# Experts' weights in pieces of 2 MB with 16 KB contiguous on a partition, in place of 1 MB with 8 KB

## The chip, the cores and the metric

The kernel runs on one core of one Trainium2 chip. Its time is the device time of one execution in microseconds (us). A profile is one further execution, taken with the hardware profiler on. In what follows MB means 1024 x 1024 bytes where a piece is meant (the profile's GB/s are decimal).

## The reference

One inference step of a small hybrid network on 256 tokens (128 of a prompt, 128 of a sample), model width 1024, one layer, all in float32. First a mixer (one input projection, a state-space scan in two directions, a convolution branch, gates, an output projection), then a mixture of 32 experts, of which each token takes 4:

```python
logits = t @ w_router + b_router                    # t: 256 x 1024
top_vals, top_idx = lax.top_k(logits, 4)
probs = softmax(top_vals)
combine = (one_hot(top_idx, 32) * probs[..., None]).sum(axis=1)
for e in range(32):
    g, u = split(t @ w_gu[e] + b_gu[e], 2)          # w_gu[e]: 1024 x 2048, 8 MB
    g = minimum(g, 7.0)
    u = clip(u, -7.0, 7.0)
    act = (u + 1.0) * g * sigmoid(1.702 * g)
    out = act @ w_down[e] + b_down[e]               # w_down[e]: 1024 x 1024, 4 MB
    acc = acc + combine[:, e:e + 1] * out
```

and at last a normalisation of both streams. The experts' weights are 32 x 12 = 384 MB and are read once.

## The kernel before

**Stages.** The mixer comes first. Its weights, some 80 MB, are loaded in pieces whose contiguous runs are 1, 2 or 8 KB; each is split in two for a product in three parts. Then the router picks the experts, and a loop `expert(e)` goes over the 32 experts. TensorE's part of that loop is written by hand in order; the other engines' order and SP's order of loads come from a scheduler.

**One expert.** A place in a list of up to 64 tokens is worked out for each expert. `gather` (line 1200) picks the tokens of two experts by products with 0/1 matrices, so that the contraction index lies on partitions: chunk `k` of eight holds 128 of the 1024 inputs. `expert_up` (line 1223, tile `e..pgu`) multiplies chunk `k` by the 128 rows of `w_gu` that belong to it, for k = 0 to 7, four products of 512 columns for each k. `expert_act` makes the activation, `transposed` (line 1272, `e..pat`) puts it on partitions in eight chunks, and `down_products` (line 1283, `e..py`) multiplies these by the rows of `w_down`. `scatter_pair` and `add_pair` bring two experts' results back to their tokens. In iteration e the order on TensorE is: down of e-1, overflow of e, up of e, then either `add_pair` or the next `gather`. `overflow` runs only for an expert with more than 64 tokens, in passes of 32 tokens (tiles `r..` and `q..`); in the profile it ran once, for expert 11.

**Pieces and places.** Twelve pieces of 1 MB make an expert: pieces 0 to 7 are 128 rows of `w_gu` each (8 KB of a row on each partition), pieces 8 to 11 are 256 rows of `w_down` (two rows of 4 KB, contiguous, on each partition). There are `NSLOT = 22` places of 1 MB, taken in turn: piece n goes where piece n-22 was, and its load waits until TensorE has read that piece. 19 places lie in memory that the mixer frees bit by bit (`open_slots`), two where a mixer buffer `y` was, one where `xn` was. `early_pieces` starts ten loads during the mixer's last products. All loads of weights are issued by SP, one after the other, so a load that waits holds back every load behind it; `load_pieces(12 * e + NSLOT)` (line 1424) sets how far ahead they are written. Down products of piece c read `w[8 + k // 2][:, k % 2]`, up products `w[k][:, 0]`.

Of the kernel before, what the change touches and what calls it, by code (L numbers as in the profile page):

```python
# [28 lines left out]
OVER = 32  # L29
NSLOT = 22  # L30
NBLOCK = 113
# [32 lines left out]
def hybrid_step(ctx, tc, A):  # L64
# [296 lines left out]

    mx, npc, ready, two = [], [0], {}, [None]
    npc_ins, last_early = [None], [None]
    w_gu, w_dn = A["w_gu"], A["w_down"]

    def next_slot(name):
        npc[0] += 1
        return slot((npc[0] - 1) % NSLOT, name)

    def slot(i, name):  # L370
        if i == NSLOT - 1:
            return keep.tile([P, 2 * D], F32, name=name, tag="xn", bufs=1)
        if i < NSLOT - 3:
            return mx[i].tile([P, 2 * D], F32, name=name, tag="w")
        if i == NSLOT - 3:
            two[0] = ypool.tile([P, 2, 2 * D], F32, name=name, tag="y")
        return two[0][:, i - (NSLOT - 3)]

    def load_piece(e, c, t=None):
        if t is None:  # L380
            t = ready.pop((e, c), None)
            if t is not None:
                npc[0] += 1
                return t
            t = next_slot(f"w{e}_{c}")
        if c < 8:
            npc_ins[0] = nc.sync.dma_start(t, w_gu[0, e, c * P:(c + 1) * P, :])
            return t.unsqueeze(1)

        t = t.rearrange("p (k n) -> p k n", k=2)  # L390
        nc.sync.dma_start(t, w_dn[0, e, (c - 8) * 256:(c - 7) * 256, :].rearrange("(p k) n -> p k n", k=2))
        return t

    def open_slots(n):
        for i in range(len(mx), len(mx) + n):
            mx.append(ctx.enter_context(tc.tile_pool(name=f"mx{i}", bufs=1, side="right")))

    def early_pieces(n):

        with tc.issue_after(last_load[0].ins):  # L400
            for _ in range(n):
                i = early.pop(0)
                ready[divmod(i, 12)] = load_piece(*divmod(i, 12), slot(i, f"w{i // 12}_{i % 12}"))
                last_early[0] = npc_ins[0]


    early = [0, 1, 2, NSLOT - 3, NSLOT - 2, *range(3, NSLOT - 3)]

    loads = [0]
    pieces = {}  # L410

    def load_pieces(n):

        for i in range(loads[0], min(n, 12 * NE)):
            pieces.setdefault(i // 12, []).append(load_piece(i // 12, i % 12))
        loads[0] = max(loads[0], n)

    first_in = []

    def weight_blocks():  # L420
# [34 lines left out]
        for c in range(8):  # L455

            w = load(f"wso{c}", w_so[:, c // 4 * KC:(c // 4 + 1) * KC, c % 4 * 256:(c % 4 + 1) * 256])
            early_pieces({2: 1, 3: 2, 5: 2}.get(c, 0))
            yield from w
        for c in range(4):  # L460

            w = piece(ring(), f"wcf{c}", w_cf[:, c // 2 * 4:c // 2 * 4 + 4, c % 2 * 512:(c % 2 + 1) * 512], [P, 4, 512])
            early_pieces(c // 3)
            w = w.rearrange("p k (i n) -> p i k n", n=P)
            yield w[:, 0:2]
            yield w[:, 2:4]
        for c in range(4):
            with tc.issue_after(last_early[0].ins) if c == 1 else ExitStack():
                w = load(f"wo{c}", w_o[:, :, c * 256:(c + 1) * 256])
            early_pieces(c // 3)  # L470
            yield from w
# [467 lines left out]

    open_slots(3)  # L940

# [4 lines left out]
    def ssd_out(hf):  # L946
        for j in range(KC):
            o = pos[j // 2][:, j % 2 * T:(j % 2 + 1) * T]
            proj(o, yhl[hf][:, 0], yhl[hf][:, 1], first=hf == 0 and j % 2 == 0, last=hf == 1)
            if hf == 1:  # L950
                V.scalar_tensor_tensor(gt[:, j, :], gt[:, j, :], 1.0, o, op0=ALU.add, op1=ALU.mult)
            if hf == 1 and j == 1:
                early_pieces(2)
            yield

    run(ssd_out(0))
    sy[0].close()
    open_slots(2)
    ssd_q.append(split_conf())
# [4 lines left out]
    sy[1].close()  # L964
    open_slots(2)
    early_pieces(1)
# [20 lines left out]
    sc.close()  # L987
    open_slots(1)
    for j in range(KC):
# [148 lines left out]
    weights.close()  # L1138
    open_slots(NSLOT - 5 - len(mx))
    hp = ctx.enter_context(tc.tile_pool(name="hp", bufs=1, side="right"))  # L1140
# [23 lines left out]

    open_slots(NSLOT - 3 - len(mx))
    def add_gated(k, s, x):
# [44 lines left out]
    def expert_up(e, xg, w, banks, m, after=None, half_way=None):  # L1211


        nq = P // m
        wd = D // nq
        for k in range(KC):
            if half_way and k == KC // 2 - 1:
                half_way()
            with tc.issue_after(after.ins) if after else ExitStack():
                for i in range(2):  # L1220
                    for q in range(nq):
                        c0 = i * D + q * wd
                        PE.matmul(banks[i][m * q:m * q + m, 0:wd], xg[:, k, :], w[k][:, 0, c0:c0 + wd],  # L1223
                                  start=(k == 0), stop=False, skip_group_check=True)
        for i in range(2):
            for q in range(nq):
                c0 = i * D + q * wd
                PE.matmul(banks[i][m * q:m * q + m, 0:wd], sel3[:, e:e + 1].to_broadcast([96, m]), b3[:, c0:c0 + wd],
# [36 lines left out]
    def transposed(gm, name, m, tag="aT", bufs=1):  # L1265

        wd = D * m // P
        pat = bank("E", name + "pat", 1)[:, 0:wd]
        aT = sm.tile([P, 512], F32, name=name + "aT", tag=tag, bufs=bufs)[:, 0:wd]
        for c in range(wd // P):  # L1270
            c0 = c // 2 * 256
            PE.transpose(pat[:, c * P:(c + 1) * P], gm[:, c0 + c % 2:c0 + 256:2], ident)  # L1272
        S.copy(aT, pat)
        return [aT[:, a:a + m] for a in (k * P % wd + k * P // wd * m for k in range(KC))]

    def down_products(at, w, py, m, swap):
# [62 lines left out]
    def overflow_pass(e, w, over, n, xo):  # L1339
# [14 lines left out]
        for c in range(wd // P):  # L1354
            PE.transpose(pxt[:, c * P:(c + 1) * P], xs[:, c * P:(c + 1) * P], ident)
        S.copy(xo, pxt[:, 0:wd].rearrange("p (c q s) -> p q c s", q=nq, s=m))
# [48 lines left out]
    def expert(e):  # L1405
        nonlocal w, last, mores
        w = pieces.setdefault(e, [])
        if e <= 1:
            load_pieces(12 * e + 12)
        if e % REGS == 0:  # L1410
# [8 lines left out]
        if e > 1:  # L1419
# [3 lines left out]

            load_pieces(12 * e + NSLOT)
        overflow(e, w, more)
# [23 lines left out]
    def finale():  # L1449
# [131 lines left out]
```

## Time and profile before

| | |
|---|---|
| Median of 3 runs | 1448.36 us (1447.45 to 1451.06) |
| The profiled execution's own time | 1453.59 us |
| Its span in the profile | 1451.8 us |
| TensorE busy | 1343.5 us (93%) |
| DMA over the span | 349 GB/s, 506.57 MB (decimal) |
| Loads of `w_gu` and `w_down` | 256 and 128, 1024 KB each |

The profiled execution lies 5.2 us above the median of the runs; sums below are made against its span, and carried to the median as differences. [...] The row of 40 slices shows the stages: the mixer up to about slice 13, then the experts, in which DMA moves some 417 GB/s slice after slice.

### The profile page before, as it was taken

The page shows a single profiled execution, that of the slowest core. Times are in us where ns is not written, and L with a number is a line of the kernel's source. Part 1 is how long each engine was busy: PE and PEld are TensorE (multiplying, and loading weights), DVE is VectorE, ACT ScalarE, POOL GpSimd, SP SyncE. Part 2 cuts the span into 40 slices and gives each one's busy share as a digit, 9 for nine tenths or more (in the row PEclk, how much of TensorE's full clock was granted, in tenths as well). Part 3 has the DMA queues.
Part 4 walks back from the last instruction along what each step waited for, and adds up shares of the span by engine and source line. Part 5 has one row for each costly group of instructions (what it writes and reads, how often), then busy time and mean ns, then how long its engine had stood idle before and what let it go on. Part 6 is the DMA issues. An engine that isn't in the chain of part 4 may idle for free. (4 is left out here: it accounts for less than half of the span.)

```text
span 1451.8 us, 21213 instructions
## 1 busy us (share of the span) xinstructions
PE 1343.5 (93%) x8531; PEld 791.8 (55%) x8531; DVE 591.1 (41%) x1265; ACT 337.5 (23%) x636; POOL 107.4 (7%) x121
## 2 busy tenths in 40 slices
PE   6898999999999899999999799999999998999986
PEld 3887888898999543443434344344344333343332
DVE  4855789898776322132122212213213213132123
ACT  2534565565664110000000000001001000000001
POOL 1112313431002100000000000000000000000001
PEclk9999999999999899999999999999999999999997
DMA  9996656556878799999999999999999999999991
GB/s 367 264 277 167 222 205 238 202 212 207 312 289 290 275 402 418 418 418 418 417 418 419 414 416 418 417 418 419 418 418 417 417 412 417 414 412 417 413 404 40
DMA packets 108625, 506.57 MB, mean 349 GB/s; under 512 B 9634, under 2 KB 36898, under 8 KB 54178
## 3 DMA queue, kind: packets, MB, share of 16 engines
q1 hardware_dynamic: 105570, 497.72, 88.0%
q10 hardware_dynamic: 2880, 6.60, 1.3%
q8 instruction: 99, 1.62, 0.5%
q14 instruction: 76, 0.62, 0.1%
HBM read 498.26 MB, written 5.64 MB: 347 GB/s over the span
## 5 line engine op out<-in xcount | busy, mean ns | idle before, releaser
L291 DVE TENSOR_TENSOR wl<-win,wh 128x1024 fp32r<-128x1024 f32 (+1 forms) x84 | 100.7, 1210 | 37.8 <-ACT wh L290 29.8
L290 ACT CAST wh<-win 128x1024 fp32r<-128x1024 f32 (+1 forms) x84 | 84.0, 1010 | 73.2 <-PE pbc L318 16.8
L1475 POOL TENSOR_TENSOR sql<-sql 128x256 f32<-128x256 f32 x3 | 2.2, 729 | 952.9 <-PE pcl L1462 952.5
L702 POOL TENSOR_TENSOR m<-m_half,adt 128x512 fp32r<-128x512 f32 x32 | 42.5, 1346 | 89.3 <-PE pss L705 89.3
L318 PE MATMUL pxs<-hT,wh 128*128 128x256 f32 x256 | 37.5, 291 | 0.0
L318 PE MATMUL pz<-hT,wh 128*128 128x256 f32 x256 | 37.3, 291 | 0.0
L318 PE MATMUL pgt<-hT,wh 128*128 128x256 f32 x256 | 36.0, 287 | 0.9 <-ACT wh L290 0.9
L318 PE MATMUL pbc<-hT,wh 128*128 128x256 f32 x256 | 35.6, 287 | 0.0
L318 PEld LDWEIGHTS pxs<-hT,wh 128*128 128x128 f32 x256 | 32.5, 190 | 3.6 <-issue 2.8
L318 PE MATMUL pso<-yhl,wh 128*128 128x256 f32 x256 | 34.1, 284 | 0.0
L318 PEld LDWEIGHTS pz<-hT,wh 128*128 128x128 f32 x256 | 33.0, 193 | 1.8 <-issue 1.8
L318 PEld LDWEIGHTS pgt<-hT,wh 128*128 128x128 f32 x256 | 32.4, 191 | 2.9 <-issue 1.9
L318 PEld LDWEIGHTS pbc<-hT,wh 128*128 128x128 f32 x256 | 32.1, 190 | 1.9 <-issue 1.7
L318 PEld LDWEIGHTS pso<-yhl,wh 128*128 128x128 f32 x256 | 32.1, 192 | 0.0
L318 PE MATMUL pglu<-hT,wh 128*128 128x256 f32 x192 | 25.9, 285 | 0.0
L318 PEld LDWEIGHTS pglu<-hT,wh 128*128 128x128 f32 x192 | 24.0, 191 | 0.7 <-issue 0.5
L215 PE MATMUL pm<-ada,sc__170 128*32 128x512 f32 x80 | 14.7, 792 | 10.0 <-DMA ada<-in_w_ada 10.0
L291 DVE TENSOR_TENSOR wl<-wso,wh 128x1024 fp32r<-128x1024 f32 x16 | 19.4, 1218 | 7.5 <-ACT wh L290 7.3
L685 ACT ACTIVATE gd<-gm,dtT 128x128 f32<-128x128 f32 x64 | 20.8, 414 | 4.3 <-DVE gm L676 4.3
L686 DVE SCALAR_TENSOR_TENSOR gd<-gm,dtT,gd 128x128 f32<-128x128 f32 x64 | 20.9, 374 | 1.6 <-ACT gd L685 1.2
L563 PE MATMUL pcv<-im,wst 128*32 128x144 f32 x256 | 12.1, 333 | 9.5 <-DMA im<-dru 5.9
L290 ACT CAST wh<-wso 128x1024 fp32r<-128x1024 f32 x16 | 16.7, 1046 | 14.4 <-PE pso L318 10.8
(1026 smaller groups left out, 2639.4 us busy)
## 6 DMA issues: line engine op xcount, KB each, us to landing
w<-in_w_gu SPq DMA_DIRECT2D x256, 1024.0 KB, 19.9
w<-in_w_down SPq DMA_DIRECT2D x128, 1024.0 KB, 19.9
win<-in_w_in_pack SPq DMA_DIRECT2D x38, 1024.0 KB, 5.6
ada<-in_w_ada SPq DMA_DIRECT2D x10, 1024.0 KB, 10.2
wso<-in_w_ssd_out SPq DMA_DIRECT2D x8, 1024.0 KB, 7.2
im<-dru SPq DMA_DIRECT2D x16, 312.0 KB, 9.2
wcf<-in_w_conf_out SPq DMA_DIRECT2D x4, 1024.0 KB, 8.8
wo<-in_w_o SPq DMA_DIRECT2D x4, 1024.0 KB, 9.2
```

The lines of the kernel that those rows point to most:

```text
L215: PE.matmul(out[32 * j:32 * j + 32, :], sc_[:, 4 * r + j, 6 - 2 * c:38 - 2 * c], part[:, j, :], start=(start and r == 0), stop=(stop and r ...
L290: S.copy(hi[:, ks, 0:m], w[:, ks])
L291: V.tensor_tensor(lo[:, ks, 0:m], w[:, ks], hi[:, ks, 0:m], ALU.subtract)
L318: last_wo[0] = PE.matmul(out, w[:, k, 0:n], m[:, k, :], start=first and i == 0, stop=last and i == len(order) - 1, skip_group_check=True)
L563: PE.matmul(pc[32 * b:32 * b + 32, h * NOUT:(h + 1) * NOUT], wst[:, 4 * h + b, j, :], im[:, 8 * (t % 2) + 4 * h + b, 4 * j:4 * j + NOUT], ...
L685: S.activation(gd[s][:, h, :], gm[:, 0, s, :], AF.Copy, scale=dtT[:, 0, s, c0:c0 + 1])
L686: V.scalar_tensor_tensor(gd[s][:, h, :], gm[:, 1, s, :], dtT[:, 0, s, 32 + c0:33 + c0], gd[s][:, h, :], op0=ALU.mult, op1=ALU.add)
L702: G.tensor_tensor(m4[d], m_half[:, d, None, None, :].to_broadcast([P, 2, 4, 64]), ac[d], ALU.mult)
L1475: G.tensor_tensor(sq[:, 0], sq[:, 0], sq[:, k], ALU.add)
```

## The change

A unit is now 2 MB, and an expert has six: four of 256 rows of `w_gu`, two of 512 rows of `w_down`. Partition p holds rows 2p and 2p+1 of the unit (or rows 4p to 4p+3 of `w_down`), which are 16 KB contiguous in HBM and on the partition. There are `NUNIT = 11` places of 2 MB. One of them, place 10, is made of two separate places of 1 MB, so that a unit that falls on it (17 of the 192) is loaded in two halves, 8 KB contiguous each. The last two units of the last expert are loaded in two halves each, too. Nine MB are started early instead of ten. Since a partition now holds neighbouring rows, the contraction index is dealt out otherwise: `gather` reads every second column of `h2`, `transposed` every fourth of the activation, and the overflow pass deals its quarters in the order 0, 2, 1, 3 and transposes with eight products of 64 x 64 in place of two of 128 x 128.

```diff
-NSLOT = 22
+NUNIT = 11
...
-    def load_piece(e, c, t=None):
...
-        if c < 8:
-            npc_ins[0] = nc.sync.dma_start(t, w_gu[0, e, c * P:(c + 1) * P, :])
-            return t.unsqueeze(1)
-
-        t = t.rearrange("p (k n) -> p k n", k=2)
-        nc.sync.dma_start(t, w_dn[0, e, (c - 8) * 256:(c - 7) * 256, :].rearrange("(p k) n -> p k n", k=2))
-        return t
...
+    def place(i, name, h):
+
+        if i < NUNIT - 2:
+            return mx[i + 1].tile([P, 4 * D], F32, name=name, tag="w")
+        if i == NUNIT - 2:
+            return ypool.tile([P, 4 * D], F32, name=name, tag="y")
+        if h:
+            return keep.tile([P, 2 * D], F32, name=f"{name}b", tag="xn", bufs=1)
+        return mx[0].tile([P, 2 * D], F32, name=f"{name}a", tag="w")
+
+    def load_unit(u, h):
+
+        e, c = divmod(u, 6)
+        src, k = (w_gu[0, e, 256 * c:256 * c + 256], 2) if c < 4 else (w_dn[0, e, 512 * (c - 4):512 * (c - 3)], 4)
+        src = src.rearrange("(p k) n -> p k n", k=k)
+        t = place(u % NUNIT, f"w{e}_{c}", h)
+        if u % NUNIT == NUNIT - 1:
+            k //= 2
+            src = src[:, h * k:h * k + k]
+        t = t.rearrange("p (k n) -> p k n", k=k)
+
+        step = k // 2 if e == NE - 1 and c > 3 else k
+        for i in range(0, k, step):
+            npc_ins[0] = nc.sync.dma_start(t[:, i:i + step], src[:, i:i + step])
+        return [t[:, i] for i in range(k)]
...
-    early = [0, 1, 2, NSLOT - 3, NSLOT - 2, *range(3, NSLOT - 3)]
+    early = [(NUNIT - 1, 0), (0, 0), (NUNIT - 2, 0), (1, 0), (2, 0)]
...
-                        c0 = (4 * q + k0 + k) * P
-                        PE.matmul(pgx[:, k * n:(k + 1) * n], h2[:, s, c0:c0 + P], g1[:, s],
+                        c0 = (4 * q + k0 + k) // 2 * 256
+                        PE.matmul(pgx[:, k * n:(k + 1) * n], h2[:, s, c0 + k % 2:c0 + 256:2], g1[:, s],
...
-                        PE.matmul(banks[i][m * q:m * q + m, 0:wd], xg[:, k, :], w[k][:, 0, c0:c0 + wd],
+                        c0 = i * D + part[q] * wd
+                        PE.matmul(banks[i][m * q:m * q + m, 0:wd], xg[:, k, :], w[k][:, c0:c0 + wd],
...
+                if n == P:
+                    PE.transpose(pat[:, i * n:(i + 1) * n], gm[:, i::4], ident)
+                else:
+                    PE.matmul(pat[r, i * n:(i + 1) * n], gm[r, i::4], ident[r, r], start=True, stop=True, skip_group_check=True)
...
-                last = PE.matmul(py[m * q:m * q + m, 0:wd], at[k], w[8 + k // 2][:, k % 2, c0:c0 + wd],
+                last = PE.matmul(py[m * q:m * q + m, 0:wd], at[k], w[KC + k][:, c0:c0 + wd],
...
-            load_pieces(12 * e + NSLOT)
+            load_pieces(6 * e + NUNIT)
```

On ScalarE, VectorE and GpSimd the instructions stand in the order in which they stood. On SP the loads change. First, the loads that stand between the early ones and the first expert's branch; in the names the number behind `w_` is that of the piece (or unit) within its expert. Before:

```order
L391 DMA w_9_5923<-in_w_down 128x2048
L391 DMA w_10_5925<-in_w_down 128x2048
L391 DMA w_8_5921<-in_w_down 128x2048
L391 DMA w_11_5927<-in_w_down 128x2048
L387 DMA w_0_6443<-in_w_gu 128x2048
L387 DMA w_1_6445<-in_w_gu 128x2048
L387 DMA w_2_6447<-in_w_gu 128x2048
L387 DMA w_3_6449<-in_w_gu 128x2048
L387 DMA w_4_6451<-in_w_gu 128x2048
L387 DMA w_5_6453<-in_w_gu 128x2048
L387 DMA w_6_6455<-in_w_gu 128x2048
L391 DMA w_9_6457<-in_w_down 128x2048
```

And now:

```order
L390 DMA w_4_5887<-in_w_down 128x4096
L390 DMA w_3_5885<-in_w_gu 128x4096
L390 DMA w_5_5889<-in_w_down 128x4096
L390 DMA w_0_6417<-in_w_gu 128x4096
L390 DMA w_1_6419<-in_w_gu 128x4096
L390 DMA w_2_6421<-in_w_gu 128x4096
L390 DMA w_4b<-in_w_down 128x2048
```

Twelve loads of 1 MB have become six of 2 MB and one of 1 MB, and the second half of the first expert's first product (unit 3) comes in here, where pieces 0 to 7 were all loaded before.

On TensorE the products are the same in number and order; what changes is which of them read one tile. This is the start of the up products of expert 2. Before:

```order
L1223 MATMUL e2pgu_7438<-w_0_6998,xg_6946 64x512 x2
L1223 MATMUL e2pgu_7439<-w_0_6998,xg_6946 64x512 x2
L1223 MATMUL e2pgu_7438<-w_1_7000,xg_6946 64x512 x2
L1223 MATMUL e2pgu_7439<-w_1_7000,xg_6946 64x512 x2
L1223 MATMUL e2pgu_7438<-w_2_7002,xg_6946 64x512 x2
L1223 MATMUL e2pgu_7439<-w_2_7002,xg_6946 64x512 x2
L1223 MATMUL e2pgu_7438<-w_3_7004,xg_6946 64x512 x2
L1223 MATMUL e2pgu_7439<-w_3_7004,xg_6946 64x512 x2
```

And now:

```order
L1224 MATMUL e2pgu_7407<-w_0_6974,xg_6922 64x512 x2
L1224 MATMUL e2pgu_7408<-w_0_6974,xg_6922 64x512 x2
L1224 MATMUL e2pgu_7407<-w_0_6974,xg_6922 64x512 x2
L1224 MATMUL e2pgu_7408<-w_0_6974,xg_6922 64x512 x2
L1224 MATMUL e2pgu_7407<-w_1_6976,xg_6922 64x512 x2
L1224 MATMUL e2pgu_7408<-w_1_6976,xg_6922 64x512 x2
L1224 MATMUL e2pgu_7407<-w_1_6976,xg_6922 64x512 x2
L1224 MATMUL e2pgu_7408<-w_1_6976,xg_6922 64x512 x2
```

A place is read by twice as many products now before it can be loaded anew.

The loads of the last expert on SP, from its predecessor's last pieces on. Before:

```order
L391 DMA w_10_21905<-in_w_down 128x2048
L391 DMA w_11_21907<-in_w_down 128x2048
L387 DMA w_11_21907<-in_w_gu 128x2048
L387 DMA w_1_21910<-in_w_gu 128x2048
L387 DMA w_2_21912<-in_w_gu 128x2048
L387 DMA w_3_21914<-in_w_gu 128x2048
L387 DMA w_4_21916<-in_w_gu 128x2048
L387 DMA w_5_21918<-in_w_gu 128x2048
L387 DMA w_6_21920<-in_w_gu 128x2048
L387 DMA w_7_21922<-in_w_gu 128x2048
L391 DMA w_8_21924<-in_w_down 128x2048
L391 DMA w_9_21926<-in_w_down 128x2048
```

And now:

```order
L390 DMA w_5_21916<-in_w_down 128x4096
L390 DMA w_0a<-in_w_gu 128x2048
L390 DMA w_0b<-in_w_gu 128x2048
L390 DMA w_1_21922<-in_w_gu 128x4096
L390 DMA w_2_21924<-in_w_gu 128x4096
L390 DMA w_3_21926<-in_w_gu 128x4096
L390 DMA w_4_21928<-in_w_down 128x2048 x2
```

The last rows of `w_gu` come as one unit of 2 MB (`w_3`), and `w_down` in halves (`w_4`, and `w_5` behind the next branch).

## Rows read from the trace of the kernel before

**Rows 1.** The page: span, the 40 slices, instruction queue, the two weight loads.
```profile
span 1451.8 us, 21213 instructions
...
GB/s 367 264 277 167 222 205 238 202 212 207 312 289 290 275 402 418 418 418 418 417 418 419 414 416 418 417 418 419 418 418 417 417 412 417 414 412 417 413 404 40
...
q8 instruction: 99, 1.62, 0.5%
...
w<-in_w_gu SPq DMA_DIRECT2D x256, 1024.0 KB, 19.9
w<-in_w_down SPq DMA_DIRECT2D x128, 1024.0 KB, 19.9
```

**Rows 2.** The chain that ended last: start us, us, what.
```profile
1072.23 20.89 DMA w<-in_w_gu
...
1114.11 19.86 DMA w<-in_w_gu
...
1338.54 6.31 DMA w<-in_w_down
...
1397.81 20.83 DMA w<-in_w_gu
1418.68 1.94 PE e31pgu L1223 x8
...
1425.66 9.35 PE e31py L1283 x32
```

**Rows 3.** Waits of SP's queue: us in total, times, longest.
```profile
SPq L387 <- DMA w<-in_w_down: 208.2, 98, 3.2
```

**Rows 4.** DMA, 1400 to 1440 us in 40 slices of 1 us.
```profile
GB/s 426 418 434 410 393 442 401 426 385 426 426 410 418 287 246 156 74 25 25 25 33 25 25 25 25 33 25 25 0 0 0 0 0 0 0 0 0 0 0 0
```

**Rows 5.** DMA, 437.5 to 443 us, pieces of 1 KB (line 469, `wo`).
```profile
DMA packets 1880, 1.91 MB, mean 347 GB/s; under 512 B 29, under 2 KB 1879, under 8 KB 1879
```

**Rows 6.** DMA, 15 to 22 us, pieces of 2 KB (line 131, `ada`).
```profile
DMA packets 1217, 2.72 MB, mean 389 GB/s; under 512 B 144, under 2 KB 144, under 8 KB 1217
```

**Rows 7.** DMA, 600 to 700 us, pieces of 8 KB (experts' weights).
```profile
DMA packets 5732, 41.80 MB, mean 418 GB/s; under 512 B 637, under 2 KB 637, under 8 KB 637
```

**Rows 8.** Busy time by stretch at the first experts (last: clock, DMA share, GB/s).
```profile
490.00:496.00 6.00, 3.87 (x13) 1.93 (x14) 1.83 (x8) 0.29 (x3) 0.00 (x0) 0.50 0.07 23
496.00:500.00 4.00, 4.00 (x14) 1.20 (x12) 0.00 (x0) 0.00 (x0) 0.00 (x0) 0.70 0.45 162
500.00:510.00 10.00, 10.00 (x56) 4.51 (x54) 0.00 (x0) 0.37 (x1) 0.00 (x0) 1.00 1.00 375
510.00:520.00 10.00, 9.50 (x64) 5.76 (x60) 4.49 (x11) 1.16 (x3) 0.00 (x0) 1.00 1.00 408
520.00:530.00 10.00, 9.28 (x46) 3.27 (x43) 0.00 (x0) 0.58 (x1) 0.00 (x0) 1.00 0.98 385
```

**Rows 9.** TensorE in order of time, first expert: start us, us.
```profile
493.13 7.95 PE L1223 MATMUL e0pgu<-w,xg 128*64 128x512 f32 x24 [2.13 <-PEq L1328]
...
523.15 7.09 PE L1283 MATMUL e0py<-w,e0aT 128*64 128x512 f32 x32 [0.72 <-ACT e0aT L1273]
```

**Rows 10.** TensorE in order of time, experts 2 to 4.
```profile
551.96 13.95 PE L1223 MATMUL e2pgu<-w,xg 128*64 128x512 f32 x64 [0.29 <-PEq L1328]
...
579.61 0.66 PE L1259 MATMUL pst<-ident,sg 128*128 128x128 f32 x4
580.55 13.96 PE L1223 MATMUL e3pgu<-w,xg 128*64 128x512 f32 x64 [0.28 <-PEq L1328]
...
594.87 3.84 PE L1200 MATMUL xg4p<-g,h 128*128 128x128 f32 x32
598.54 0.64 PE L1272 MATMUL e3pat<-ident,e3gm 128*128 128x128 f32 x4
...
607.24 1.08 PE L1223 MATMUL e4pgu<-w,xg 128*64 128x512 f32 x4 [0.29 <-PEq L1328]
```

**Rows 11.** SP's queue in order of time, 816 to 829 us.
```profile
817.57 10.97 SPq L391 DMA_DIRECT2D w<-in_w_down  x2
```

More of the change, by code (lines that the diff above doesn't have):

```diff
@@ L359, in hybrid_step @@
     w_o = A["w_o"].rearrange("l (k p) n -> p (l k) n", p=P)
-    mx, npc, ready, two = [], [0], {}, [None]
+    mx, nun, ready = [], [0], {}
     npc_ins, last_early = [None], [None]
     w_gu, w_dn = A["w_gu"], A["w_down"]
[L366 to L377, printed above, removed]
@@ L379, in load_piece @@
-    def load_piece(e, c, t=None):
[L380 to L383, printed above, removed]
-                return t
-            t = next_slot(f"w{e}_{c}")
-        if c < 8:
-            npc_ins[0] = nc.sync.dma_start(t, w_gu[0, e, c * P:(c + 1) * P, :])
-            return t.unsqueeze(1)
-        t = t.rearrange("p (k n) -> p k n", k=2)
-        nc.sync.dma_start(t, w_dn[0, e, (c - 8) * 256:(c - 7) * 256, :].rearrange("(p k) n -> p k n", k=2))
-        return t
@@ L394, in open_slots @@
-    def open_slots(n):
-        for i in range(len(mx), len(mx) + n):
-            mx.append(ctx.enter_context(tc.tile_pool(name=f"mx{i}", bufs=1, side="right")))
+    def place(i, name, h):
[6 more added lines that the diff above has]
+        return mx[0].tile([P, 2 * D], F32, name=f"{name}a", tag="w")
@@ L398, in early_pieces, with parts, open_places @@
+    def parts(u):
+        return range(2 if u % NUNIT == NUNIT - 1 else 1)
+    def open_places(*sizes):
+        for n in sizes:
+            mx.append(ctx.enter_context(tc.tile_pool(name=f"mx{len(mx)}", bufs=1, side="right")))
     def early_pieces(n):
@@ L401, in early_pieces @@
             for _ in range(n):
-                i = early.pop(0)
-                ready[divmod(i, 12)] = load_piece(*divmod(i, 12), slot(i, f"w{i // 12}_{i % 12}"))
+                u, h = early.pop(0)
+                ready[u, h] = load_unit(u, h)
                 last_early[0] = npc_ins[0]
-    early = [0, 1, 2, NSLOT - 3, NSLOT - 2, *range(3, NSLOT - 3)]
-    loads = [0]
+    early = [(NUNIT - 1, 0), (0, 0), (NUNIT - 2, 0), (1, 0), (2, 0)]
     pieces = {}
     def load_pieces(n):
-        for i in range(loads[0], min(n, 12 * NE)):
-            pieces.setdefault(i // 12, []).append(load_piece(i // 12, i % 12))
-        loads[0] = max(loads[0], n)
+        for u in range(nun[0], min(n, 6 * NE)):
+            for h in parts(u):
+                pieces.setdefault(u // 6, []).extend(ready.pop((u, h), None) or load_unit(u, h))
+        nun[0] = max(nun[0], n)
     first_in = []
@@ L457, in weight_blocks @@
             w = load(f"wso{c}", w_so[:, c // 4 * KC:(c // 4 + 1) * KC, c % 4 * 256:(c % 4 + 1) * 256])
-            early_pieces({2: 1, 3: 2, 5: 2}.get(c, 0))
+            early_pieces({2: 1, 3: 1, 5: 1}.get(c, 0))
             yield from w
@@ L462, in weight_blocks @@
             w = piece(ring(), f"wcf{c}", w_cf[:, c // 2 * 4:c // 2 * 4 + 4, c % 2 * 512:(c % 2 + 1) * 512], [P, 4, 512])
-            early_pieces(c // 3)
             w = w.rearrange("p k (i n) -> p i k n", n=P)
@@ L469, in weight_blocks @@
                 w = load(f"wo{c}", w_o[:, :, c * 256:(c + 1) * 256])
-            early_pieces(c // 3)
             yield from w
@@ L938, in split_conf @@
             yield
-    open_slots(3)
+    open_places(1, 2)
     pos = [bank("A", f"pso{j}", 3) if j < 6 else bank("B", f"pso{j}", 1) for j in range(0, KC, 2)]
@@ L952, in ssd_out @@
             if hf == 1 and j == 1:
-                early_pieces(2)
+                early_pieces(1)
             yield
@@ L957, in hybrid_step @@
     sy[0].close()
-    open_slots(2)
+    open_places(2)
     ssd_q.append(split_conf())
@@ L964, in hybrid_step @@
     sy[1].close()
-    open_slots(2)
+    open_places(2)
     early_pieces(1)
@@ L987, in hybrid_step @@
     sc.close()
-    open_slots(1)
     for j in range(KC):
@@ L1138, in hybrid_step @@
     weights.close()
-    open_slots(NSLOT - 5 - len(mx))
+    open_places(*[2] * 5)
     hp = ctx.enter_context(tc.tile_pool(name="hp", bufs=1, side="right"))
@@ L1163, in hybrid_step @@
     sm = ctx.enter_context(tc.tile_pool(name="sm", bufs=1))
-    open_slots(NSLOT - 3 - len(mx))
+    open_places(2)
     def add_gated(k, s, x):
@@ L1215, in expert_up @@
         wd = D // nq
+        part = (0, 1) if nq == 2 else (0, 2, 1, 3)
         for k in range(KC):
@@ L1226, in expert_up @@
             for q in range(nq):
-                c0 = i * D + q * wd
+                c0 = i * D + part[q] * wd
                 PE.matmul(banks[i][m * q:m * q + m, 0:wd], sel3[:, e:e + 1].to_broadcast([96, m]), b3[:, c0:c0 + wd],
@@ L1267, in transposed @@
         wd = D * m // P
+        n = wd // 4
         pat = bank("E", name + "pat", 1)[:, 0:wd]
         aT = sm.tile([P, 512], F32, name=name + "aT", tag=tag, bufs=bufs)[:, 0:wd]
-        for c in range(wd // P):
-            c0 = c // 2 * 256
-            PE.transpose(pat[:, c * P:(c + 1) * P], gm[:, c0 + c % 2:c0 + 256:2], ident)
+        for i in range(4):
+            for r in range(0, P, n):
+                r = slice(r, r + n)
+                if n == P:
+                    PE.transpose(pat[:, i * n:(i + 1) * n], gm[:, i::4], ident)
+                else:
+                    PE.matmul(pat[r, i * n:(i + 1) * n], gm[r, i::4], ident[r, r], start=True, stop=True, skip_group_check=True)
         S.copy(aT, pat)
-        return [aT[:, a:a + m] for a in (k * P % wd + k * P // wd * m for k in range(KC))]
+        return [aT[:, i * n + h * m:i * n + h * m + m] for h in range(2) for i in range(4)]
     def down_products(at, w, py, m, swap):
@@ L1354, in overflow_pass @@
         for c in range(wd // P):
-            PE.transpose(pxt[:, c * P:(c + 1) * P], xs[:, c * P:(c + 1) * P], ident)
+            PE.transpose(pxt[:, c * P:(c + 1) * P], xs[:, c::2], ident)
         S.copy(xo, pxt[:, 0:wd].rearrange("p (c q s) -> p q c s", q=nq, s=m))
@@ L1408, in expert @@
         if e <= 1:
-            load_pieces(12 * e + 12)
+            load_pieces(6 * e + 6)
         if e % REGS == 0:
@@ L1453, in finale @@
         products = pair_products(sT[NE - 2], y)
-        sq = next_slot("sql").rearrange("p (k t) -> p k t", t=T)
+        sq = place(6 * NE % NUNIT, "sql", 0)[:, 0:2 * D].rearrange("p (k t) -> p k t", t=T)
         def finish(c):
```

1 line of the change is left out of this document (removed).

## The prediction

> **What bounds the kernel now.** I read the page's row of 40 slices first, then the chain, then the DMA of single stretches. From about 505 us to 1412 us DMA moves 415 to 420 GB/s in nearly every slice [rows 1], so the expert stage runs at the pace of its loads. The chain says the same of the end: from 1072 to 1418 us it is almost only loads of weights, in steps that span eight loads [rows 2]. That is how many are in flight: a load takes 19.9 us to land [rows 1], a 1 MB piece comes every 2.5 us, and SP waits for its own earlier loads (some 200 us in this row, and there are three such) [rows 3]. From 1072.23 to 1338.54 us there are 13 steps, so a step takes 20.49 us and a piece **2.56 us**; a step is either 19.9 or 20.9 us long.
>
> The mean of all engines, 418 GB/s, would be 2.51 us per piece. The end shows why the chain is slower. After 1413 us the rate falls, and from 1417 to 1427 us it is 25 GB/s, a sixteenth of the whole [rows 4]: one DMA engine is still working, alone, some 12 us behind the others. A load has landed only when its last sixteenth has, so this engine paces the chain. The steps that are 1.0 us longer fit a 16 KB instruction packet that it carries in between: 99 of these packets take 0.5% of 16 engines' span, 1.2 us each [rows 1]. They are not changed. (That they all run on the late engine isn't shown; it enters no term below.)
>
> TensorE is not the bound. From the up products of expert 2 to those of expert 4 it needs 607.24 - 551.96 = 55.3 us with hardly a wait [rows 10], where 24 pieces need 24 x 2.56 = 61.5 us. Only near the start, with all 22 places full, and after expert 11's overflow pass is SP held by places that TensorE has not freed.
>
> **The change part by part.** *Cost of a packet.* Each DMA engine moves a piece as packets of one contiguous run. At 1 KB a run the 16 engines give 347 GB/s, at 2 KB 389, at 8 KB 418 [rows 5 to 7]; so a packet takes 16 x 1024 / 347 = 47.2 ns, 84.2 ns and 313.6 ns. A line through the first and the last has 38.1 ns per KB and a fixed 9.1 ns, and would give 85.3 ns at 2 KB; a line through the last two has a fixed 7.7 ns. A 16 KB packet saves one fixed part for every 16 KB. An engine's share of 1 MB is 64 KB, so that is four fixed parts, 31 to 36 ns, and half of one completion packet of at most another 8 to 9 ns: **35 to 41 ns per MB**, and I take 38, 1.5% of 2.56 us.
>
> [...]
>
> *How many pieces gain.* 384 MB, less 22 that fill the places before the first product, is 362. Sixteen later units fall on the split place 10 and come in halves with 8 KB runs: 32 MB gain nothing, nor do the last 4 MB. That leaves 326 MB x 38 ns = **12.4 us** (11.4 to 13.4).
>
> *The start.* The mixer's loads keep their order, and 1 MB less is started early. That costs nothing: before the first expert all places fill up and DMA stands nearly idle (0.07 busy at 23 GB/s from 490 to 496 us [rows 8]), which is 6 us of cover where 1 MB needs 2.5. But the loads begin again when a place comes free. That was after one k of the first expert, 7.95 / 3 = 2.65 us [rows 9], and is now after two: **2.65 us** later, with DMA idle. Then the first expert's down products free 1 MB after two of eight k, 2 x 7.09 / 8 = 1.8 us, before, and 2 MB after 3.5 us now. Before, DMA ran short there already (375, 408, 385 GB/s against 418 from 500 to 530 us, 2.1 us lost [rows 8]); up to 1.8 us more is lost. Together 2.65 to 4.4, I take **3.5 us**. Each us is paid in full, since the loads are the chain to the end.
>
> *The end.* The last rows of `w_gu` come as 2 MB, four MB ahead of the end as before. When they land TensorE has two k left instead of one, 1.94 us more [rows 2]. `w_down` comes in halves of 1 MB as before, and its products (9.35 us) begin late enough to find it landed. **1.9 us**.
>
> *TensorE's other strides.* `gather` reads its weights at a stride of two, which `transposed` did already. Four transposes at a stride of two take 0.64 us, four at a stride of one (`pst`) 0.66 us [rows 10]: no cost. A stride of four has no row; it lies between nothing and, say, a doubling of the 0.64 us, and `pat` is nearest to nothing. Eight small products in an overflow pass add at most as much, once. All of it is covered by the 61.5 - 55.3 = 6.2 us that TensorE has to spare on two experts; without that cover it would be 0.64 us an expert, 20 us in all.
>
> *Loads half as many.* Waits for the landing, 19.9 us, double with the size. That is hidden as long as loads stay in flight. [...] The chain's 2.49 us per piece with eight in flight [rows 2] shows it hidden already, so this sum takes nothing for it.
>
> **Sum.** -12.4 + 3.5 + 1.9 = -7.0 us: span 1444.8, the profiled execution 1446.6 against 1453.59, the median **1441.4** against 1448.36. From the bounds, -13.4 + 4.6 = -8.8 and -11.4 + 6.3 = -5.1. I call 0.3% (4.3 us) the least change a measurement of this kernel can tell.
>
> **The rivals.**
> *A, the rate stays.* Above 8 KB the engine, or the memory behind it, may move bytes at 418 GB/s whatever the run. For it: the fixed part is read from loads of other tensors, whose short runs may be slow for other reasons. Against: the three sizes lie on one line within 1.5%. Then only the coarser grain is left, +5.4 us: 1453.8. It decides where 326 MB gain less than 5.4 us, 17 ns per MB, a 16 KB packet at more than 623 ns.
> *B, half the gain.* If half of the fixed part overlaps with the transfer of a long run, 17 of the 35 ns are left, and 326 x 17 ns = 5.5 us are gained and spent again: 1448.3. [...]
> *C, full places at expert 11.* SP issued nothing from 817.57 until a place came free at 828 us (two loads, 10.97 us [rows 11]). The last load before the gap was 19.9 us from landing, so some 9 us of work was left. With loads 1.5% faster over 320 us (4.8 us ahead, less the 3.5 us lost at the start) and another 13.95 / 8 = 1.74 us until two k free a place [rows 10], some 6 us should be left. If not, the engines stop, and all gain before 830 us is void: the rest is 12.4 x 590 / 930 = 7.9, net -2.5: 1445.9.
> *D, no loss at the start*, because the late engine has work while the others wait: -12.4 + 1.9, 1437.9.
> *E, the new run is slow.* The only 16 KB packets in the trace take 1.2 us, twice the 0.62 us that I forecast; neighbouring partitions also now lie 16 KB apart in HBM. At 1% slower, 9 us and the 5.4: 1463 or more. Against: those packets carry instructions, not weights.
> [...]
>
> **How the numbers follow.** Chances: forecast 0.52 (1439.5 to 1444.5), A 0.13, B 0.11, C 0.11, D 0.07, E 0.06. The range 1436 to 1454 reaches from beyond D to A and leaves out E and the edges of A. Faster than 1444.0: nine tenths of the forecast, D, and a little of C, 0.56. Slower than 1452.7: A and E and a little of B, 0.19. The rest, 0.25, is the same.
>
> **What would show it.** Right: 425 GB/s where the slices show 418; chain steps of some 40 us for eight loads, 5.05 us per 2 MB; loads begin again at 499 us; 1.9 us longer from the last `w_gu` to the end. Wrong: a rate still at 418 (A) or between (B), a dip in the slice at 830 us that lasts more than 2 us (C), TensorE with waits for nothing while `pat` or `gather` last longer. Wrong too if the late engine isn't the bound: if the others, 12 us ahead, catch up with places first.

## The result and the profile after

The changed kernel takes **1442.23 us** (median of 7 runs, 1439.95 to 1443.64), the kernel before 1449.52 us (7 runs, 1447.45 to 1451.06): a ratio of 0.9945, 95% interval 0.9936 to 0.9955. That is 7.3 us less by the medians and 8 us by the ratio. The forecast was 1441.4.

The page of the changed kernel: span, the row of 40 slices, the two queues of instructions, and the two bulk loads with their median time to landing.

```profile
span 1440.0 us, 20912 instructions
...
GB/s 367 275 275 175 217 211 236 206 211 205 312 289 264 274 401 425 424 423 426 422 426 425 413 419 425 422 426 425 424 425 424 426 423 427 422 426 424 425 369 37
...
q8 instruction: 100, 1.64, 0.5%
q14 instruction: 73, 0.60, 0.1%
...
w<-in_w_gu SPq DMA_DIRECT2D x116, 2048.0 KB, 30.3
w<-in_w_down SPq DMA_DIRECT2D x57, 2048.0 KB, 26.3
```

Where the row of before had 418 in slice after slice [rows 1], this one has 422 to 427, and its last but one slice is down to 369 where 404 stood. The same stretch as [rows 7], 600 to 700 us:

```profile
DMA packets 3205, 42.45 MB, mean 425 GB/s; under 512 B 355, under 2 KB 355, under 8 KB 355
```

There are 2850 long packets in place of 5095, for more bytes. 1 MB takes 1048576 B / 425 GB/s = 2.467 us where it took 2.508: **41 ns less per MB** by the whole GB/s, and 38 by the bytes of the two rows (42.45 against 41.80 MB). This is a mean over all units, those loaded in two halves of 8 KB runs among them.

The chain that ended last (start us, us, what) answers to [rows 2]:

```profile
1187.18 13.96 PE e24pgu L1224 x64
...
1213.74 9.70 PE e24py L1290 x32
1223.45 35.68 DMA w<-in_w_down
1259.20 35.32 DMA w<-in_w_down
1294.59 36.74 DMA w_1a<-in_w_gu
1331.39 38.74 DMA w<-in_w_gu
1370.20 35.24 DMA w<-in_w_gu
1405.48 3.65 PE e31pgu L1224 x16
...
1413.80 8.70 PE e31py L1290 x32
```

The steps of loads now begin at 1223 us, where those of before ran through at 1072 already; ahead of them stand TensorE's products of expert 24, which had to free the place. Five steps take 182.0 us, 36.4 us each. That fits eight loads: but for the halves of the last two units, 192 units come as 209 loads, 1.84 MB on average, and 8 x 1.84 x 2.467 = 36.3. From the landing of the last `w_gu` to the end of the span are 1440.0 - 1405.48 = 34.5 us, against 33.1 [rows 1] [rows 2] (32.2 in a second profile of the kernel before).

TensorE's waits from 1000 to 1420 us (engine, line, waited for: us in total, times, longest):

```profile
PE e27pgu L1224 <- PEq L1335: 2.5, 1, 2.5
PE e19pgu L1224 <- PEq L1335: 2.3, 1, 2.3
PE e31pgu L1224 <- DMA w<-in_w_gu: 1.5, 2, 1.2
```

Two things are new. TensorE waits for weights only at the last expert, 1.5 us; before, it did so at experts 24, 30 and 31 (3.1, 3.0 and 1.7 us), among others. And it stands for 2.3 and 2.5 us at a branch (line 1335 is the test for an overflow pass; PEq is its own sequencer), where before no wait at that branch behind the first experts was longer than 0.7 us. The kernel before has one stall of this length, too, but inside the products of expert 25 (2.77 us, in brackets below), and the profile names nothing that it waits for:

```profile
1235.21 13.08 PE L1223 MATMUL e25pgu<-w,xg 128*64 128x512 f32 x52 [2.77 <-issue]
```

The start, by stretches of equal distance from TensorE's first expert product, which is at 490.36 us here and at 493.13 us in [rows 9] (last three columns: granted clock, DMA share, GB/s):

```profile
490.36:500.36 10.00, 10.00 (x42) 4.52 (x44) 0.18 (x2) 0.07 (x1) 0.00 (x0) 0.75 0.32 95
500.36:510.36 10.00, 10.00 (x53) 3.85 (x51) 1.11 (x2) 0.63 (x2) 0.00 (x0) 1.00 1.00 397
510.36:520.36 10.00, 9.03 (x54) 5.10 (x53) 3.38 (x10) 1.42 (x4) 0.00 (x0) 1.00 0.97 398
520.36:530.36 10.00, 9.98 (x48) 3.41 (x50) 0.69 (x1) 0.58 (x1) 0.00 (x0) 1.00 0.97 381
...
490.36:550.36 60.00, 57.82 (x296) 26.06 (x298) 9.35 (x20) 5.46 (x11) 0.00 (x0) 0.96 0.88 354
```

The same 60 us of the kernel before, and of a second profile of it:

```profile
493.13:553.13 60.00, 57.80 (x298) 26.01 (x300) 9.36 (x19) 5.46 (x11) 0.00 (x0) 0.96 0.92 367
```

```profile
489.09:549.09 60.00, 57.80 (x300) 26.10 (x302) 9.53 (x20) 5.46 (x11) 0.00 (x0) 0.96 0.92 370
```

Measured against each kernel's own full rate, the loads lose 60 - 60 x 354 / 425 = 10.0 us of these 60 now and lost 60 - 60 x 367 / 418 = 7.3 before (6.9 in the second profile): **2.7 to 3.1 us** more. From 540 us on DMA is full until 1390 us (425 GB/s up to 820 us, 424 from 835 us on), but for one dip at expert 11's overflow pass:

```profile
820.00:825.00 5.00, 3.83 (x68) 1.67 (x58) 2.00 (x8) 0.37 (x1) 0.00 (x0) 1.00 0.97 410
825.00:830.00 5.00, 5.00 (x26) 1.76 (x24) 2.76 (x11) 0.00 (x0) 0.00 (x0) 1.00 0.84 318
830.00:835.00 5.00, 5.00 (x26) 1.80 (x24) 0.00 (x0) 0.00 (x0) 0.00 (x0) 1.00 1.03 433
```

107 GB/s are missing over 5 us, 1.3 us; before, the lowest was 387, which is 0.4 us:

```profile
830.00:835.00 5.00, 4.19 (x20) 1.93 (x21) 0.53 (x2) 0.00 (x0) 0.00 (x0) 1.00 0.96 387
```

**How spans are compared below.** In two profiles of the kernel before, the first expert's products begin at 493.1 and at 489.1 us though nothing differs: the mixer's time scatters by some us. So I also give the stretch from TensorE's first expert product to the end of the span. It is 958.7 and 957.9 us in the two profiles of before and 949.6 us in that of after.

### The profile page after: what moved, and what is told of

The parts are those of the page before. It is cut to its first block, busy times and chain, and to the rows that moved or that the text cites. A ratio compares the mean times of both kernels' runs of the same rounds, so it can differ in the third digit from the quotient of the medians.

```text
span 1440.0 us, 20912 instructions
## 1 busy us (share of the span) xinstructions
PE 1341.3 (93%) x8545; PEld 795.8 (55%) x8545; DVE 591.6 (41%) x1265; ACT 337.8 (23%) x636; POOL 110.2 (8%) x121
## 5 line engine op out<-in xcount | busy, mean ns | idle before, releaser
L318 PEld LDWEIGHTS pbc<-hT,wh 128*128 128x128 f32 x256 | 32.2, 190 | 1.9 <-issue 1.7
L290 ACT CAST wh<-wso 128x1024 fp32r<-128x1024 f32 x16 | 16.7, 1045 | 14.3 <-PE pso L318 10.8
L318 PE MATMUL pwo<-mhl,wh 128*128 128x256 f32 x128 | 18.9, 290 | 0.2 <-DVE mhl L996 0.2
## 6 DMA issues: line engine op xcount, KB each, us to landing
w<-in_w_gu SPq DMA_DIRECT2D x116, 2048.0 KB, 30.3
w<-in_w_down SPq DMA_DIRECT2D x57, 2048.0 KB, 26.3
```

What stands on the lines that cost most here:

```text
L290: S.copy(hi[:, ks, 0:m], w[:, ks])
L318: last_wo[0] = PE.matmul(out, w[:, k, 0:n], m[:, k, :], start=first and i == 0, stop=last and i == len(order) - 1, skip_group_check=True)
```

## The experiments

Ten kernels ran beside the changed one. What they gave, each as a ratio to runs of the kernel before that were made beside it, and with the rate from 600 to 700 us of each profile (before: 418 GB/s; after: 425):

| kernel | run of a packet, load | GB/s | first expert to end, us | ratio to before (95%) |
|---|---|---|---|---|
| after | 16 KB, 2 MB | 425 | 949.6 | 0.9945 (0.9936 to 0.9955) |
| run8_2m | 8 KB, 2 MB | 419 | 960.9 | 1.0022 (1.0004 to 1.0040) |
| run8_1m | 8 KB, 1 MB | 418 | 960.0 | 1.0010 (0.9991 to 1.0029) |
| run16_1m | 16 KB, 1 MB | 424 | 955.0 | 0.9971 (0.9950 to 0.9993) |
| run4_1m | 4 KB, 1 MB | 409 | 987.8 | 1.0208 (1.0170 to 1.0246) |
| half_loads | 16 KB, 2 MB | 207 | 941.3 | 0.9864 (0.9832 to 0.9896) |
| last_gu_halves | 16 KB, 2 MB | 424 | 947.1 | 0.9934 (0.9911 to 0.9957) |
| split_first | 16 KB, 2 MB | 424 | 951.2 | 0.9962 (0.9947 to 0.9977) |
| one_pass | 16 KB, 2 MB | 424 | 1005.6 | 1.0289 (1.0275 to 1.0303) |
| before_again | 8 KB, 1 MB | 418 | 957.9 | one run, 1448.73 us |

The tenth, one_pass_halves, belongs to one_pass: 996.3 us, 1.0288 (1.0272 to 1.0304).

### The run or the size of the load?

Four kernels with the 2 MB places of after. **run8_2m** gives a unit its rows as before, in two runs of 8 KB on a partition, as one load, and TensorE the strides of before:

```diff
-        src = src.rearrange("(p k) n -> p k n", k=k)
+            src = w_gu[0, e, 256 * c:256 * c + 256].rearrange("(j p) n -> p j n", j=2)
...
+            src = w_dn[0, e, 512 * (c - 4):512 * (c - 3)].rearrange("(j p k) n -> p j (k n)", j=2, k=2)
```

> Loads of 2 MB into places of 2 MB, but each partition's 16 KB are two runs of 8 KB from two far rows, as in the kernel before (and TensorE's strides as before). If the run length makes the gain (a fixed 8 to 9 ns for each packet): 418 to 419 GB/s from 600 to 700 us, and the time of the kernel before plus the cost of the coarser places, 3.5 + 1.9 us, less at most 1.5 us for half the completions: 1453 to 1455 us. If the size of a load makes it (half as many loads, each with its fixed cost): 425 GB/s and the changed kernel's 1442 us.

**run8_1m** is after with every full unit loaded in two halves, each 8 KB of every partition:

```diff
-        step = k // 2 if e == NE - 1 and c > 3 else k
+        step = k if u % NUNIT == NUNIT - 1 else k // 2
```

> The changed kernel with every 2 MB place filled by two loads of 1 MB, each with runs of 8 KB (one of the two neighbouring rows of w_gu, or two of the four of w_down). Run length theory: 418 GB/s and 1455 us, the kernel before plus 5.4 us for the coarse places. Size theory: the same. If the coarse places cost nothing: 1449.5 us, as before.

**run16_1m** halves the loads too, but by partitions, so that runs stay at 16 KB:

```diff
+            for i in range(2):
+                npc_ins[0] = nc.sync.dma_start(t[i::2], src[i::2])
```

> The changed kernel with every 2 MB place filled by two loads of 1 MB that keep runs of 16 KB, each on every second partition. Run length theory: 425 GB/s less the second completion, 1443 to 1444 us. Size theory: 418 GB/s, 1455 us. If a load on 64 partitions is spread badly over the engines: far slower than both, and then it decides nothing.

**run4_1m** halves them by every second row of 4 KB (or half a row of 8 KB):

```diff
+                x, y = (z[:, i::2] if k == 4 else z[:, :, i * D:(i + 1) * D] for z in (t, src))
+                npc_ins[0] = nc.sync.dma_start(x, y)
```

> The changed kernel with every 2 MB place filled by two loads of 1 MB with runs of 4 KB (half a row of w_gu, every second row of w_down on a partition); the split place and the last two units stay as they are. Run length theory, with the fixed 7.7 to 9.1 ns for each packet: 406 to 408 GB/s, 326 MB x 62 to 73 ns = 20 to 24 us over the same with 8 KB runs, 1475 to 1479 us. Size theory: as with 8 KB runs, 1455 us.

DMA from 600 to 700 us in run8_2m, run8_1m, run16_1m and run4_1m, one row each:

```profile
DMA packets 5449, 41.85 MB, mean 419 GB/s; under 512 B 348, under 2 KB 348, under 8 KB 348
```

```profile
DMA packets 5734, 41.83 MB, mean 418 GB/s; under 512 B 635, under 2 KB 635, under 8 KB 635
```

```profile
DMA packets 3492, 42.43 MB, mean 424 GB/s; under 512 B 644, under 2 KB 644, under 8 KB 644
```

```profile
DMA packets 10073, 40.91 MB, mean 409 GB/s; under 512 B 624, under 2 KB 624, under 8 KB 9549
```

The rate follows the run and hardly the load: 418 and 419 at 8 KB, 424 and 425 at 16 KB. Per packet on one of 16 engines that is 16 x 4096 / 409 = 160.2 ns at 4 KB, 313.6 at 8 KB, 616.8 at 16 KB; two packets less one of twice the size leave a fixed 6.8 and 10.4 ns, around the 7.7 to 9.1 of the prediction. The medians were 1453.46 us for run8_2m (1453 to 1455 had been expected), 1452.51 for run8_1m (1455), 1445.66 for run16_1m (1443 to 1444) and 1481.71 for run4_1m (1475 to 1479): the order is that of the runs' lengths, and all but the first miss their numbers by some 2 to 3 us. run8_2m and run8_1m also price the coarse places alone: 960.5 us from the first expert to the end against 958.3, **2.2 us** (1.3 to 3.0 by single profiles), where the prediction had 5.4. In run8_1m the last rows of `w_gu` come in halves, so that it has no loss at the end to show.

run16_1m has the rate of after and still stands 5.4 us behind it. Its chain, from expert 31 on, names no load:

```profile
1401.00 13.95 PE e31pgu L1228 x64
...
1419.61 8.81 PE e31py L1294 x32
```

TensorE sets its end: in that profile it stood before experts 7 and 23 at a branch (2.2 and 2.5 us) and before 15 and 25 for what the profile puts down to a load (2.5 and 2.8 us). At expert 15 that can't be, since the load that it names, `w_2a`, brings weights of expert 16; below, all four turn out to be of one kind. The loads of run16_1m also lose more at expert 11 than those of after: 265 and 218 GB/s in two stretches of 5 us, some 4.3 us against 1.3. So the rate alone doesn't make the gain. Why its stalls fall at other experts than those of after isn't settled.

### What is left of the loads?

**half_loads**: from expert 2 on, every odd expert uses the weights of the expert before it and loads none.

```diff
+                if u >= 12 and u // 6 % 2:
+                    if u % 6 == 5:
+                        pieces.setdefault(u // 6, []).extend(pieces[u // 6 - 1])
+                    continue
```

> The changed kernel without the loads of the odd experts from 3 on: each multiplies by the weights of the expert before it, which are still in place (part of the computation is changed, the products are the same in number and order). Loads fall to 17 of 32 experts, so TensorE alone sets the pace. If loads still bound the changed kernel, as forecast, the time falls by 7 us or more, to TensorE's 55.3 us for two experts: 1435 us or less. If TensorE already bounds it nearly everywhere, it falls by the 1.5 us for which TensorE still waits for loads at the end, at most 4 us: 1438 to 1441 us.

Its time is 0.9864 of before, 0.8% or 12 us under after; from the first expert to the end it takes 941.3 us, 8.3 less than after. That part is the cleaner measure, since the runs of this kernel scatter (1427.89 to 1438.49). DMA is at half rate (700 to 1000 us), and the last expert's products wait for nothing:

```profile
700.00:1000.00 300.00, 278.87 (x1566) 121.75 (x1564) 72.86 (x196) 25.21 (x45) 0.00 (x0) 0.99 0.52 212
```

```profile
1392.40 13.95 PE e31pgu L1232 x64
...
1411.02 8.81 PE e31py L1298 x32
```

So 941.3 us is what TensorE needs by itself here. The kernel before stood 17 us above that (958.3), after stands 8.3 above: half of what lay between is taken. The stalls before experts 19 and 27 are gone as well, though the products are the same in number and order; that wait at expert 19 is 0.3 us. Whether they go with the traffic of the loads isn't shown: half as many loads to issue and to wait for change the engines' programs as well (its trace has 17 fewer records of TensorE's instructions than that of after). What the stalls cost in after is seen in its windows at expert 19 (the clock is the third number from the end):

```profile
1040.00:1045.00 5.00, 5.00 (x27) 1.64 (x22) 0.00 (x0) 0.22 (x1) 0.00 (x0) 1.00 0.99 416
1045.00:1050.00 5.00, 2.73 (x11) 0.94 (x11) 1.29 (x3) 0.94 (x2) 0.00 (x0) 0.84 1.02 424
1050.00:1055.00 5.00, 5.00 (x22) 1.65 (x20) 0.00 (x0) 0.00 (x0) 0.00 (x0) 0.82 1.02 429
1055.00:1060.00 5.00, 5.00 (x26) 1.71 (x24) 0.00 (x0) 0.00 (x0) 0.00 (x0) 1.00 0.99 423
```

Behind the 2.3 us gap the granted clock is 0.84 and 0.82 in two stretches (in steps of 1 us it is 1.00 up to 1048 us, then 0.69, 0.50, 0.50 and 0.60, and 1.00 again from 1052 us on), and the up products take 15.7 us in place of 13.95. From the start of expert 12 to that of 24 TensorE takes 336.7 us, in half_loads 333.0; the 2.5 us before expert 27 came without a slower clock. Together some 6 of the 8.3 us.

That spoils half_loads as a test of what it was to tell. The time fell by more than 7 us, which stood for loads that still bound the changed kernel, but most of the fall is the stalls, which neither case had. With its stalls TensorE alone would need some 941.3 + 6 = 947 us, so after stands only 2 us above its own TensorE: loads and TensorE now end almost together.

### The end and the start

**last_gu_halves** loads the last unit of `w_gu` in two halves too:

```diff
-        step = k // 2 if e == NE - 1 and c > 3 else k
+        step = k // 2 if e == NE - 1 and c > 2 else k
```

> The changed kernel with the last 2 MB of w_gu of the last expert loaded in two halves as well. Forecast: the second-last k is done while the last lands, 1.9 us less. If TensorE is as late there by itself, less: 0 to 1 us.

Measured: 1440.17 us (6 runs), ratio 0.9934 against 0.9945; the intervals overlap. From the first expert to the end 947.1 against 949.6 us, and from expert 31's first product 45.0 against 46.8: **1.8 us** at the end, as the end's term of 1.9 said, seen in one execution each. Of the versions that leave nothing of the reference out it is the fastest that ran, though not surely faster than after.

**split_first** makes place 0 of two places of 1 MB, so that the loads begin again after one k of the first expert:

```diff
+        if i == 0:
+            return mx[1].tile([P, 2 * D], F32, name=name + "ab"[h], tag=("wa", "wb")[h])
...
-        if u % NUNIT == NUNIT - 1:
+        if u % NUNIT in (0, NUNIT - 1):
```

> The changed kernel with place 0 made of two places of 1 MB too, so that its loads begin again after one k of the first expert instead of two; 17 more units come in halves with 8 KB runs. By the prediction's working (each us at the start is paid in full): 2.65 us gained at the start, 34 MB x 41 ns = 1.4 us given back in rate, 1.2 us less in all (ratio 0.9937). Rival, that the delay at the start is hidden by the other places' loads: only the 1.4 us remain, slower by that much (0.9955). In the trace the first reload is issued 3.7 us behind the first product instead of 6.1 in either case; what tells is the length from the first expert's start to the end: 949.6 us now, 948.4 by the first, 951 by the second.

By its length from the first expert to the end (951.2 us) and its ratio it is the rival: nothing is gained. The windows, from its first expert product on:

```profile
487.77:497.77 10.00, 10.00 (x42) 4.54 (x44) 0.35 (x2) 0.28 (x1) 0.00 (x0) 0.77 0.54 195
497.77:507.77 10.00, 10.00 (x54) 4.05 (x51) 1.29 (x2) 0.64 (x3) 0.00 (x0) 1.00 0.81 306
507.77:517.77 10.00, 8.99 (x54) 5.07 (x55) 3.20 (x9) 1.19 (x4) 0.00 (x0) 1.00 0.97 390
...
487.77:547.77 60.00, 57.99 (x298) 26.20 (x300) 9.60 (x20) 5.46 (x11) 0.00 (x0) 0.96 0.88 353
```

The first 10 us move 1 MB more than after (195 against 95 GB/s), the next 10 us 0.9 MB less (306 against 397), and over 60 us both stand at the same 353 and 354. The loads began 2.5 us earlier, but the unit behind them waits for its own two k as before (issued 11.6 us behind the first product, 11.8 in after), and DMA runs dry there instead.

### Does TensorE's time count now?

**one_pass** leaves out the inner branch and its hint, to shorten TensorE's program and move the stalls:

```diff
-            tc.mark_branch_hint_location(f"more{e}", "LikelyTaken", ALL)
...
-            with tc.If(more > 1, label=f"more{e}"):
-                with tc.For_i(1, more, 1):
-                    overflow_pass(e, w, over, f"q{e}", xo)
```

> The changed kernel without the branch for overflow passes beyond the first (left out: passes that an expert with more than 96 tokens would need; in this input no expert runs them). TensorE's program gets shorter, so that the places in it at which TensorE stood 2.3 and 2.5 us before experts 19 and 27 should shift or go; those stalls and the slow products behind them were 6 us. Theory 'the loads still set the end': DMA had no idle time from 530 to 1390 us, so what TensorE gains it waits for loads later on; time 0 to 1.5 us under the changed kernel (ratio 0.9935 to 0.9945), and TensorE's waits for w_gu grow from 1.5 us to some 6. Theory 'TensorE sets the end since the change': 4 to 6 us less (ratio 0.990 to 0.992). If the stalls stay, it tells nothing of either.

Neither theory's number came: 1492.72 us, 2.9% slower. The stalls did not go; they came before 24 of the 31 later experts, like this one (TensorE in order of time; in brackets the idle time ahead and what ended it):

```profile
1174.01 15.65 PE L1224 MATMUL e22pgu<-w,xg 128*64 128x512 f32 x64 [2.10 <-PEq L1335]
```

and the page shows more large and fewer small transfers of instructions than after:

```profile
q8 instruction: 125, 2.05, 0.6%
q14 instruction: 37, 0.30, 0.1%
```

The waits at line 1335 of over 1 us sum to 50.3 us with the first expert's. The stretch from the first expert to the end is 1005.6 us, 64 over TensorE's own 941.3: 49 us of stalls after the first expert, 6.5 us of three more inside the products of experts 8, 15 and 26, and slower products behind several. As a test of what sets the end of after it fails, since it made TensorE far slower than the loads. It does show that a stall at the branch depends on what stands in the program around it.

The transfers of instructions tell more. In one_pass a packet of 16 KB begins 2.6 to 2.7 us before the products go on at each of these 24 stalls, whether the stall lasts 1.0 or 2.9 us, and lands 1.5 to 1.7 us before; it begins 2.4 to 2.6 us before at the three inside products. So it is in after at both stalls (2.8 us; the row below is of 1044 to 1045 us, where expert 19's products begin at 1047.58), in run8_1m at both (2.9), in run16_1m at all four, those put down to a load among them (2.9 to 3.0), and at the stall in expert 25 of the kernel before (2.6). Of the 28 experts from 2 on that have no long stall in after, one begins its products so soon behind such a packet (expert 2, after 0.5 us of waiting); in run16_1m and run8_1m none does.

```profile
q8 instruction: 1, 0.02, 6.4%
```

This fits a TensorE that waits for its own code. That these packets carry TensorE's code is in no row, and no run changed them alone.

**one_pass_halves** is one_pass with the edit of last_gu_halves:

> The kernel without passes beyond the first (as in one_pass), and with the last unit of w_gu loaded in two halves. If the loads set the end: the two gains are those of each alone, 1.6 us for the halves and 0 to 1.5 for the passes, ratio 0.992 to 0.9935. If TensorE sets the end: the halves give nothing beside one_pass, and both stand at 0.990 to 0.992.

It stands at 1492.07 us, one_pass at 1492.72: where TensorE sets the end, the halves give nothing that can be seen, as its second case said, though nearly 4% above that case's numbers.

**before_again** is the kernel before, profiled a second time.

> The kernel before, profiled once more, to see how much of the difference of the two profiled executions (11.8 us in the span) is the execution's own: whether the first expert's products begin at 493 us again, or at 490 us as in the changed kernel.

Its span is 1447.0 us against 1451.8. Of the 11.8 us between the spans of [rows 1] and of after, 2.8 lay ahead of the first expert (493.1 against 490.4 us), where the two profiles of the kernel before differ by 4.0 among themselves.

## Why the prediction was right, step by step

**The bound.** Right, with less room than it said. DMA has hardly an idle moment (417 GB/s from 700 to 1000 us, 415 from 1072 to 1338) and TensorE waits for weights at experts 24, 30 and 31 of the kernel before; its 17 us above TensorE's own time is the most that faster loads could take back. The prediction priced TensorE's cover at 6.2 us on two experts; over 16 such pairs that would be 99 us. But the 22 MB that lie ready at the first expert are a head start of 22 x 2.51 = 55 us, and TensorE loses some 36 us of its own: 24 in the overflow pass (53.0 us from expert 10 to 11 where such a step else takes 28.6), 8.5 at experts 24 and 25 (64.0 us for the pair in half_loads, in place of 55.5) and 4 in the first two (59 in place of 55.3). That leaves 8; what makes it 17 is, by estimate, the loads' late start (3.7 us to the first, some 2 lost behind it) and the last expert. A spare read from one pair of experts is not the spare of the stage.

**The packet.** Right in the mechanism, and a little too small. The prediction had 35 to 41 ns for each of the 326 MB that gain, and none for the others; the 38 to 41 ns measured are the mean over all 362 MB, 13.9 to 14.8 us where 12.4 (11.4 to 13.4) were taken. Rivals A (418) and B (half) are out by the rate, and E by the packet: 16 KB of weights take 617 ns, where those of instructions take 1.2 us by the rounded share in [rows 1], and 1.02 us in the row of 1044 to 1045 us above (6.4% of 16 engines in 1 us). Of the time per MB the longer run saves 1.6% from 8 to 16 KB, and 2.2% from 4 to 8 KB. The wait for a landing, which the prediction doubled with the size, grew from 19.9 us [rows 1] to 30.3 and 26.3.

**The start.** 3.5 us forecast (2.65 to 4.4), 2.7 to 3.1 measured: the size is right and rival D is out, but the reason isn't borne out. The step that failed is that each us by which the first loads begin later "is paid in full". They do begin again 2.5 us later (6.2 us after the first product, against 3.7). But split_first, which takes that delay away, loses as much: DMA runs dry 10 us later, since the unit behind waits for its own two k. So what costs is rather that the places behind come free two k at a time, and not the first delay.

**The end.** 1.4 to 2.3 us (34.5 against 33.1 and 32.2) where 1.9 was forecast; last_gu_halves, which takes the cause away, ends 1.8 us sooner behind expert 31's start.

**Expert 11.** Rival C did not come, but a small part of it did: 1.3 us of missing DMA time against 0.4. The sum had nothing for it; 0.9 us.

**The sum.** With -13.9 to -14.8, 2.7 to 3.1, 1.4 to 2.3 and 0.9 it is -7.6 to -9.8 us, and the stretch from the first expert to the end got shorter by 8.3 to 9.1. The medians fell by 7.3, the ratio's interval is 6.5 to 9.3 us. That the forecast of -7.0 stands within 0.3 of the medians is in part luck: the gain in rate came out larger, and expert 11 took some of it.

**TensorE's strides.** Costed at nothing. Gathering takes 4.04 us, where [rows 10] have 3.84:

```profile
592.49 4.04 PE L1200 MATMUL xg4p<-g,h 128*128 128x128 f32 x32
...
605.07 1.51 PE L1224 MATMUL e4pgu<-w,xg 128*64 128x512 f32 x6 [0.29 <-PEq L1335]
```

From expert 2 to expert 4 it is 605.07 - 549.58 = 55.5 us, against 55.3 [rows 10]. This is covered, as said; the cover is now nearly used up. The prediction did not see the stalls at the branch. run8_1m, with TensorE's strides of after and the rate of before, has them too (2.2 and 2.1 us, before the same experts); run8_2m, with the strides and transposes of before, has none of over 1 us at the branch behind the first expert. So they go with the program and not with the rate. Longer code to skip alone is not the reason, since one_pass has less of it and more stalls. The packets of instructions point to a wait for code; why that falls on one expert and not on another isn't settled.

**What stays open.** How much of after's remaining 8.3 us the 6 us of stalls would give back if they were gone with the loads still at full rate: one_pass was to show it and did not. Since DMA has no idle time from 540 to 1390 us but at expert 11, and TensorE waits for the last `w_gu`, it should be little; that is argued, and no run shows it.

## What to carry to other kernels

If a stage is bound by its loads, look at the length of the contiguous run before the size of the load: with some 8 loads in flight the run alone set the rate here, 409, 418 and 425 GB/s at 4, 8 and 16 KB. Before you price such a gain, find how far the next engine lies behind the loads over the whole stage (a kernel with half the loads showed it in one run), since the gain ends there: 17 us here, not the 99 that one pair of experts promised. Look in such a run for stalls that went away with the loads, which 6 of the 8.3 us were here. And price a delayed load by the DMA time that is lost over the next tens of us: here the loads behind it had to wait anyway, and an earlier first load gained nothing.

## What had not been expected of the hardware

A branch that was skipped at 31 of 32 experts cost TensorE 0.3 us at most of them in after, but behind the first expert 1.0 to 2.9 us at some: before 2 experts in after, 4 in run16_1m, 24 in one_pass, none in the kernel before, which has one such stall inside its products instead. Each of these stalls ended 2.4 to 3.0 us after a 16 KB packet of instructions began, so the count of such packets on the page (100 in after, 125 in one_pass) is worth a look when TensorE stands and nothing is named. Behind one of these gaps in after the granted clock was 0.82 to 0.84 for several us, and 64 products took 15.7 us in place of 13.95.
